# One-hot products for an expert list, and two halves of the tokens' split side by side in one 512-column matmul

## The chip, the cores and the metric

The kernel runs on one core of one Trainium2 chip. The metric is the device time of an execution in microseconds (us). Before the change it is 2601.82 us, the median of three runs (2600.1 to 2602.65).

## What is computed

Two transformer blocks over 256 tokens of width 2048, in float32. The change lies in the part `peer` of the first block, a layer of 16384 small experts: each token chooses 16 experts in each of 8 heads by its scores, takes a gelu of the product of its normed vector with each chosen row of `expert_u`, multiplies by the gates and adds up the chosen rows of `expert_v`.

```python
eidx = e1 * PEER_NKEYS + e2            # 8 heads x 16 experts for a token
gates = jax.nn.softmax(vs, axis=-1)
def block(args):                       # 128 tokens
    xb, ib, gb = args
    act = jax.nn.gelu(jnp.einsum('tkd,td->tk', expert_u[ib], xb))
    return jnp.einsum('tk,tkd->td', act * gb, expert_v[ib])
h = h + peer(rms_norm(h, ffn_norm_gain), w_pq, sub_k1, sub_k2, expert_u, expert_v)
```

## The kernel before

Nothing is gathered for U: all 16384 rows of `expert_u` are read, in 128 steps (`UStep`) of 128 experts, and multiplied with the 256 tokens. What a token hasn't chosen gets a gate of zero. For V only the experts that some token chose are read, by a list.

Float32 products are made of three products in a faster format (float32r): each operand is split into a high part (a copy by ScalarE) and a low part (a subtraction by VectorE), and high x high, high x low and low x high are added in PSUM. The tokens' parts are `xt["h"]` and `xt["l"]`, 16 blocks k of 128 channels x 256 tokens. A step of U works like this, in the order in which it is written, which is the order in which each engine works (`tc.manual_schedule`):

- `prep` of step f+1 comes ahead of the matmuls of step f (`Stream.prep`, look-ahead 1): ScalarE makes the high parts of step f+1 (L818), SyncE loads the rows of step f+2 and VectorE transposes them into `uT` (L808), and VectorE makes the low parts of step f+1 (L823). In the first 64 steps (`NFU`) 8 of the 16 blocks (`NF`) aren't split: they are multiplied in float32, each as two passes (L829). So these steps have one pair of split tiles, the later ones two.
- `mm` of step f: the float32 blocks first, then for each k three products of 256 columns (L834, L835, L836) into the first half of one of three PSUM banks (`ubank`).
- `u_finish` ends gelu for step f-1: a tanh on ScalarE (L849), the last product on VectorE (L850, it reads PSUM) and a DMA of GpSimd's queue into AG in DRAM (L851). Then the first part of gelu for step f: a square on ScalarE (L839) and a product on VectorE (L840).

The tiles `ga` come from a pool of 5 (`t1`) and are free again when their DMA has landed.

After each `mm` a background of generators gets a budget of work (`bg.run`: 2.2 in the first 64 steps, 2.0 in the others; each `yield` says what it cost). It holds, in this order: the top-16 searches for the two halves of the tokens (VectorE mostly), the gates of four groups of 64 tokens (`gate_gen`: one-hots from ScalarE and VectorE, products on TensorE, a copy by ScalarE), their stores (`store_gen`, 16 DMAs of GpSimd's queue each), and `lists_gen`.

`lists_gen` sorts the experts into four classes: chosen by the first 128 tokens alone, by both halves, by the second alone, by none. It computes each expert's place in the list on TensorE, and writes the expert's number to that place of `listD` in DRAM with 128 indirect DMAs of 128 rows (L1121), which GpSimd issues, each with a small memset behind it (L1125). Then the list is read back (L1129), transposed and kept as `listI`.

The V stage runs over blocks of 128 list entries: gathers of AG and `expert_v` by GpSimd's queue (L872, L873), splits, and matmuls of 512 columns (L896 to L898), 24 for a block that serves both halves of the tokens and 12 for one that serves one. `WA, WB0, WB1` say which blocks serve which half: blocks below WA the first, those from WB0 to WB1 the second. If the classes don't fit, a flag is set and a slow loop over the remaining blocks runs behind a `tc.If`.

Of the kernel before, what the change touches and what calls it, by code (L numbers as in the profile page):

```python
# [25 lines left out]
NE = 128  # L26
WB = 4
NF = 8
NFU = 64
WA, WB0, WB1 = 82, 27, 111  # L30

# [58 lines left out]
def tile_kernel(ctx: ExitStack, tc: tile.TileContext, A, out, dbg=None):  # L90
# [20 lines left out]
    def bank(tag):  # L111
        return psp.tile([128, 512], F32, tag=tag, name=tag)
# [155 lines left out]
    xt = {}  # L268

    def new_xt():  # L270
        xt["h"] = xp.tile([128, 16, 256], F32R, tag="xh", name="xh")
        xt["l"] = xp.tile([128, 16, 256], F32R, tag="xl", name="xl")

# [476 lines left out]
    AG = dr.tile([NE * 128, 512], F32, name="AG")  # L750
    listD = dr.tile([NE * 128, 64], F32, name="listD")
# [9 lines left out]
    G.iota(iota, pattern=[[1, 16]], base=0, channel_multiplier=0, allow_small_or_imprecise_dtypes=True)  # L761
    r_bc = tk.tile([128, 256], F32, name="r_bc")
    iotaf = tk.tile([128, 128], F32, name="iotaf")
# [9 lines left out]
    G.iota(pcol, pattern=[[0, 1]], base=0, channel_multiplier=1, allow_small_or_imprecise_dtypes=True)  # L773
    idf = tk.tile([128, 192], F32, name="idf")
    G.iota(idf, pattern=[[128, 192]], base=0, channel_multiplier=1, allow_small_or_imprecise_dtypes=True)
    posU = tk.tile([128, 128], U32, name="posU")
# [3 lines left out]
    gap = tk.tile([1, 1], F32, name="gap")  # L780
    ubank = [bank("acc") for _ in range(3)]
# [5 lines left out]
    class UStep:  # L787
# [38 lines left out]
        def mm(self):  # L826
            acc = ubank[self.f % 3][:, 0:256]
            for k in range(self.nf):
                T.matmul(acc, self.uT[:, k * 128:(k + 1) * 128], xf[:, k, :], start=(k == 0), stop=False)  # L829
            per = (16 - self.nf) // self.nw  # L830
            for k in range(self.nf, 16):
                hi, lo = self.u[(k - self.nf) // per]
                c = slice((k - self.nf) % per * 128, ((k - self.nf) % per + 1) * 128)
                T.matmul(acc, hi[:, c], xt["h"][:, k, :], start=(k == 0), stop=False)  # L834
                T.matmul(acc, hi[:, c], xt["l"][:, k, :], start=False, stop=False)  # L835
                T.matmul(acc, lo[:, c], xt["h"][:, k, :], start=False, stop=(k == 15))  # L836
            u_finish()
            a = t1(F32, "ga")
            S.activation(a, acc, AF.Square)  # L839
            V.scalar_tensor_tensor(a, a, GC1 / GC3, acc, op0=OP.add, op1=OP.mult)  # L840
            pend.append((self.f, acc, a))

    pend = []

    def u_finish():
        if not pend:
            return
        f, x, a = pend.pop()
        S.activation(a, a, AF.Tanh, scale=GC3)  # L849
        V.scalar_tensor_tensor(a, a, 1.0, x, op0=OP.add, op1=OP.mult)  # L850
        G.dma_start(AG[f * 128:f * 128 + 128, 0:256], a)  # L851

    class VStep:
# [12 lines left out]
        def prep(self):  # L866
# [12 lines left out]
            for c in range(2):  # L879
                if self.rest:  # L880
                    hi, lo = [xt[n].rearrange("p k t -> p (k t)")[:, c * 1024:(c + 1) * 1024] for n in "hl"]
# [203 lines left out]
    def lists_gen():  # L1085
# [26 lines left out]
        V.tensor_reduce(pf[:, 0:128], q.rearrange("p a b -> p b a"), AX, OP.add)  # L1112
        V.tensor_copy(posU, pf[:, 0:128])
        V.tensor_scalar(flag[:, 0:1], ps[0:1, 128:129], float(WB0 * 128), None, op0=OP.is_lt)
# [4 lines left out]
        yield 3.0  # L1119
        for f in range(NE):  # L1120
            i = G.indirect_dma_start(out=listD[:, :], out_offset=bass.IndirectOffsetOnAxis(ap=posU[:, f:f + 1], axis=0),  # L1121
                                     in_=idf[:, f:f + 64], in_offset=None)
            tc.declare_no_dep(i.ins, group="list", reason="the rows written are all different")
            tc.add_to_no_dep_group("list", i.ins)
# [422 lines left out]
    def merged_gen(i, j0, j1):  # L1547
        for j in range(j0, j1):
# [6 lines left out]
            k0 = 8 * i + 2 * j  # L1555
            split(flat(xt["h"][:, k0:k0 + 2, :]), flat(xt["l"][:, k0:k0 + 2, :]), pt)
            yield
# [38 lines left out]
```

## Time and profile before

| | before |
|---|---|
| median of 3 runs | 2601.82 us |
| the profiled execution | 2613.04 us |
| its span, from the first to the last instruction | 2611.3 us |
| TensorE busy | 2516.7 us (96%) |
| VectorE busy | 1815.7 us (70%) |
| ScalarE busy | 1315.0 us (50%) |
| GpSimd busy | 554.3 us (21%) |
| granted TensorE clock, mean | 0.986 |

In the rows TensorE is PE (its weight loads PEld), VectorE is DVE, ScalarE ACT, GpSimd POOL, SyncE SP. L834 is line 834 of the kernel. Matmuls overlap, so their durations don't add up: the distance between their starts counts. The same holds, to a lesser degree, for VectorE and ScalarE, where an instruction starts about 0.1 us before the one ahead of it ends. An idle time in brackets names what ended it; "issue" means that the profile shows nothing that the engine waited for.

### The profile page before, as it was taken

How to read it: one execution, taken by the hardware profiler on the slowest of the kernel's cores; microseconds unless marked ns; L12 is line 12 of the kernel's file. 1: busy time of each engine (PE TensorE's matmuls, PEld its weight loads, DVE VectorE, ACT ScalarE, POOL GpSimd, SP SyncE). 2: the span in 40 equal slices, each digit the busy share in tenths (PEclk: the TensorE clock that was granted, in tenths of full speed). 3: DMA queues.
4: the chain of work that ended last, by engine and by line, in shares of the span. 5: the costliest groups of instructions: out<-in, count | busy, mean ns of one | idle time of the engine just before them, and what ended most of it. 6: DMA issues, size and time to landing. Idle time of an engine off the chain costs nothing. (4 is left out here: it accounts for less than half of the span.)

```text
span 2611.3 us, 38031 instructions
## 1 busy us (share of the span) xinstructions
PE 2516.7 (96%) x13895; PEld 2195.1 (84%) x13896; DVE 1815.7 (70%) x2804; ACT 1315.0 (50%) x2169; POOL 554.3 (21%) x789
## 2 busy tenths in 40 slices
PE   9999989999999999998779999999999999999999
PEld 8877779899898999997668888887888888888887
DVE  5665678987979989886447777777665456754564
ACT  6764643254452577543235555555555456544443
POOL 3000000001201112388725555553000000000000
PEclk9999999999999999999789999999999999999999
DMA  6644876565757868696469989987555545555554
GB/s 220 193 129 146 193 165 167 165 168 168 220 144 201 212 176 223 181 241 192 127 241 324 320 321 318 320 317 273 189 191 187 184 163 180 190 178 193 181 193 157
DMA packets 251619, 538.63 MB, mean 206 GB/s; under 512 B 29800, under 2 KB 165952, under 8 KB 236832
## 3 DMA queue, kind: packets, MB, share of 16 engines
q1 hardware_dynamic: 206864, 344.54, 44.4%
q0 software_dynamic: 40992, 189.67, 21.2%
q10 hardware_dynamic: 3568, 1.91, 0.3%
q8 instruction: 111, 1.82, 0.3%
q14 instruction: 84, 0.69, 0.1%
HBM read 494.06 MB, written 41.94 MB: 205 GB/s over the span
## 5 line engine op out<-in xcount | busy, mean ns | idle before, releaser
L120 DVE TENSOR_TENSOR wl<-raw,wh 128x1024 fp32r<-128x1024 f32 (+4 forms) x642 | 740.3, 1171 | 375.8 <-ACT wh L119 341.3
L119 ACT ACTIVATE wh<-raw 128x1024 fp32r<-128x1024 f32 (+4 forms) x642 | 640.1, 1011 | 372.2 <-PE acc L247 279.0
L836 PE MATMUL acc<-xh,wl 128*128 128x256 f32 x1536 | 444.7, 289 | 31.0 <-DVE wl L823 20.7
L245 PE MATMUL acc<-wh,xh 128*128 128x512 f32 (+2 forms) x1152 | 456.7, 396 | 6.0 <-ACT h L406 4.2
L834 PE MATMUL acc<-xh,wh 128*128 128x256 f32 x1536 | 456.0, 297 | 6.1 <-issue 5.5
L835 PE MATMUL acc<-xl,wh 128*128 128x256 f32 x1536 | 441.6, 288 | 9.3 <-issue 8.5
L247 PE MATMUL acc<-wh,xl 128*128 128x512 f32 (+2 forms) x1152 | 447.3, 388 | 0.0
L246 PE MATMUL acc<-wl,xh 128*128 128x512 f32 (+2 forms) x1152 | 446.6, 388 | 0.3 <-DVE wl L120 0.3
L808 DVE STREAM_TRANSPOSE uT<-raw 128x2048 f32<-128x2048 f32 x128 | 295.4, 2308 | 60.5 <-PE acc L829 54.0
L836 PEld LDWEIGHTS acc<-xh,wl 128*128 128x128 f32 x1536 | 300.5, 196 | 39.2 <-DVE wl L823 26.0
L835 PEld LDWEIGHTS acc<-xl,wh 128*128 128x128 f32 x1536 | 301.2, 196 | 11.9 <-issue 10.2
L834 PEld LDWEIGHTS acc<-xh,wh 128*128 128x128 f32 x1536 | 300.9, 196 | 11.8 <-issue 9.9
L245 PEld LDWEIGHTS acc<-wh,xh 128*128 128x128 f32 x1152 | 217.5, 189 | 47.3 <-ACT h L406 4.6
L839 ACT ACTIVATE ga<-acc 128x256 f32<-128x256 f32 x128 | 49.1, 383 | 412.3 <-PE acc L836 325.0
L247 PEld LDWEIGHTS acc<-wh,xl 128*128 128x128 f32 x1152 | 217.3, 189 | 44.0
L246 PEld LDWEIGHTS acc<-wl,xh 128*128 128x128 f32 x1152 | 217.8, 189 | 41.0 <-DVE wl L120 0.7
L818 ACT ACTIVATE wh<-uT 128x1024 fp32r<-128x1024 f32 x192 | 195.1, 1049 | 87.3 <-DVE uT L808 87.2
L829 PE MATMUL acc<-xf,uT 128*128 128x256 f32 x1024 | 234.3, 382 | 3.9 <-ACT h L404 3.9
L823 DVE TENSOR_TENSOR wl<-uT,wh 128x1024 fp32r<-128x1024 f32 x192 | 224.6, 1197 | 7.6 <-ACT wh L818 7.5
L851 POOL DMA_DIRECT2D AG<-ga x128 | 71.1, 556 | 739.4 <-DVE ga L850 723.7
L829 PEld LDWEIGHTS acc<-xf,uT 128*128 128x128 f32 x1024 | 190.9, 191 | 28.2 <-ACT h L404 4.3
L872 POOL DMA_INDIRECT ag<-AG,listI x111 | 142.5, 1284 | 75.9 <-DVE pl L120 51.6
(418 smaller groups left out, 3817.4 us busy)
## 6 DMA issues: line engine op xcount, KB each, us to landing
raw<-in_expert_u_dram SPq DMA_DIRECT2D x1024, 128.0 KB
raw<-in_w_in_dram SPq DMA_DIRECT2D x96, 1024.0 KB
raw<-in_w_out_dram SPq DMA_DIRECT2D x32, 1024.0 KB
raw<-in_w_pq_dram SPq DMA_DIRECT2D x64, 256.0 KB
AG<-ga POOLq DMA_DIRECT2D x128, 128.0 KB
AG<-GB POOLq DMA_DIRECT2D x64, 256.0 KB
raw<-in_w_ple_gate_dram SPq DMA_DIRECT2D x16, 1024.0 KB
raw<-in_w_in_dram SPq DMA_DIRECT2D x16, 544.0 KB
```

The costliest lines, as they stand in the source:

```text
L119: S.activation(hi, src, AF.Copy)
L120: V.tensor_tensor(lo, src, hi.bitcast(F32), op=OP.subtract)
L245: T.matmul(o, xh, hi, start=first, stop=False)
L246: T.matmul(o, xh, lo, start=False, stop=False)
L247: T.matmul(o, xl, hi, start=False, stop=last)
L808: V.transpose(uT.rearrange("p b g j -> p g b j"), self.raw.rearrange("p g (b i) -> p g b i", i=32))
L818: S.activation(hi, self.uT[:, self.nf * 128 + i * n:self.nf * 128 + (i + 1) * n], AF.Copy)
L823: V.tensor_tensor(lo, self.uT[:, self.nf * 128 + i * n:self.nf * 128 + (i + 1) * n], hi.bitcast(F32), op=OP.subtract)
L829: T.matmul(acc, self.uT[:, k * 128:(k + 1) * 128], xf[:, k, :], start=(k == 0), stop=False)
L834: T.matmul(acc, hi[:, c], xt["h"][:, k, :], start=(k == 0), stop=False)
L835: T.matmul(acc, hi[:, c], xt["l"][:, k, :], start=False, stop=False)
L836: T.matmul(acc, lo[:, c], xt["h"][:, k, :], start=False, stop=(k == 15))
```

## The change

- **U's products.** The tokens' high and low parts lie side by side (`xt["x"]`, two tiles of 8 blocks; a class `Half` gives the old views). High part of U times both is one matmul of 512 columns, into a whole bank; low part of U times the high part follows with 256 columns into the bank's first half. The order is: all high products but the last, the float32 blocks, all low products, the last high product.
- **The halves.** ScalarE copies the second half of the bank to a tile `gx`, VectorE adds the first half to it. The square and gelu's two products then work on that tile in SBUF.
- **Gelu's last product** moves from VectorE to GpSimd, as an addition of 1 and a product.
- **Pools.** `t1` has 7 tiles for 5 (two are used per step now); `r_bc` lies in another pool.
- **The list.** The scatter through DRAM goes. An expert's place is split into a high part (block) and a low part (entry), each is made a one-hot by VectorE (comparisons of 8 x 128 columns, result in bf16), ScalarE scales one of them with the expert's row number, and 128 bf16 products on TensorE add up the row numbers in the spare half of the bank `cnt`. The other part of the expert's number, its group f, follows from how many places lie ahead of each group's experts: counts by one-hots and a triangle of ones.
- **Block counts.** `WA, WB0, WB1` are 81, 28, 110 for 82, 27, 111.

The diff, cut to its core:

```diff
-WA, WB0, WB1 = 82, 27, 111
+WA, WB0, WB1 = 81, 28, 110
...
+        xt["x"] = [xp.tile([128, 8, 2, 256], F32R, tag=t, name=t) for t in ("xh", "xl")]
+        xt["h"], xt["l"] = Half(xt["x"], 0), Half(xt["x"], 1)
...
-        return tk.tile([128, 256], dt, tag="t1", name=name, bufs=5)
+        return tk.tile([128, 256], dt, tag="t1", name=name, bufs=7)
...
         def mm(self):
-            acc = ubank[self.f % 3][:, 0:256]
+            bank = ubank[self.f % 3]
+            acc = bank[:, 0:256]
...
+            def high(k):
+                T.matmul(bank, part(k, 0), xt["x"][k // 8][:, k % 8].rearrange("p n t -> p (n t)"),
+                         start=(k == self.nf), stop=(k == 15))
+
+            for k in range(self.nf, 15):
+                high(k)
             for k in range(self.nf):
-                T.matmul(acc, self.uT[:, k * 128:(k + 1) * 128], xf[:, k, :], start=(k == 0), stop=False)
+                T.matmul(acc, self.uT[:, k * 128:(k + 1) * 128], xf[:, k, :], start=False, stop=False)
             for k in range(self.nf, 16):
-                T.matmul(acc, hi[:, c], xt["h"][:, k, :], start=(k == 0), stop=False)
-                T.matmul(acc, hi[:, c], xt["l"][:, k, :], start=False, stop=False)
-                T.matmul(acc, lo[:, c], xt["h"][:, k, :], start=False, stop=(k == 15))
+                T.matmul(acc, part(k, 1), xt["h"][:, k, :], start=False, stop=False)
+            high(15)
             u_finish()
+            u = t1(F32, "gx")
+            S.activation(u, bank[:, 256:512], AF.Copy)
+            V.tensor_tensor(u, acc, u, op=OP.add)
             a = t1(F32, "ga")
-            S.activation(a, acc, AF.Square)
-            V.scalar_tensor_tensor(a, a, GC1 / GC3, acc, op0=OP.add, op1=OP.mult)
-            pend.append((self.f, acc, a))
+            S.activation(a, u, AF.Square)
+            V.scalar_tensor_tensor(a, a, GC1 / GC3, u, op0=OP.add, op1=OP.mult)
+            pend.append((self.f, u, a))
...
         S.activation(a, a, AF.Tanh, scale=GC3)
-        V.scalar_tensor_tensor(a, a, 1.0, x, op0=OP.add, op1=OP.mult)
+        G.tensor_scalar(a, a, 1.0, None, op0=OP.add)
+        G.tensor_tensor(a, a, u, op=OP.mult)
         G.dma_start(AG[f * 128:f * 128 + 128, 0:256], a)
...
-        for f in range(NE):
-            i = G.indirect_dma_start(out=listD[:, :], out_offset=bass.IndirectOffsetOnAxis(ap=posU[:, f:f + 1], axis=0),
-                                     in_=idf[:, f:f + 64], in_offset=None)
-            G.memset(gap, 0.0)
-            if f % 5 == 4:
-                yield 2.0
-        lt = t1(F32, "lt")
-        G.dma_start(GB, listD.rearrange("(b p) o -> b p o", p=128))
-        for _ in range(4):
-            yield 2.0
-        V.tensor_copy(lt[:, 0:128], GB[:, :, 0])
-        pt = bank("ms")
-        T.transpose(pt[:, 0:128], lt[:, 0:128], ident)
-        V.tensor_copy(listI, pt[:, 0:128])
+        def hots(tag, col, n):
+            o = tk.tile([128, 8, 128], BF16, tag=tag, name=tag, bufs=3)
+            V.tensor_tensor(o[:, 0:n], iotaf[:, None, :].to_broadcast([128, n, 128]),
+                            pq[:, col:col + n][:, :, None].to_broadcast([128, n, 128]), op=OP.is_equal)
+            return o
...
+        def products(f0, oa, ob):
+            for j in range(8):
+                T.matmul(lst, ob[:, j], oa[:, j], start=(f0 + j == 0), stop=(f0 + j == NE - 1))
+
+        for f0 in range(0, NE, 8):
+            oa, ob = hots("o1", f0, 8), hots("o2", 128 + f0, 8)
+            S.activation(flat(oa), flat(oa), AF.Copy, scale=pcol)
+            if prev:
+                products(*prev)
+            prev = (f0, oa, ob)
+            yield 2.3
+        products(*prev)
+        V.scalar_tensor_tensor(hf[:, 0:128], hf[:, 128:256], 128.0, lst, op0=OP.mult, op1=OP.add)
+        V.tensor_copy(listI, hf[:, 0:128])
```

Ahead of the loop, left out here, stand some twenty small VectorE operations, two more comparisons (4 x 128 columns) and three short round trips to TensorE, parted by yields of 4.0, 4.0, 1.0 and 2.0; they give the places' two parts and each group's number.

## Rows read from the trace of the kernel before

**Rows 1.** Busy time by stretch: start:end, length, engines' busy us (instructions), clock, DMA.

```profile
399.44:562.99 163.55, 157.21 (x1009) 145.59 (x1008) 147.35 (x286) 54.09 (x103) 12.48 (x23) 1.00 0.63 170
562.99:628.86 65.87, 65.87 (x480) 62.41 (x478) 43.70 (x79) 41.70 (x98) 3.79 (x7) 1.00 0.52 139
628.86:698.52 69.66, 65.77 (x415) 60.55 (x413) 66.59 (x170) 21.80 (x41) 19.79 (x26) 1.00 0.75 219
698.52:773.05 74.53, 74.53 (x543) 70.64 (x541) 53.70 (x98) 47.74 (x113) 4.91 (x9) 1.00 0.58 155
773.05:860.59 87.54, 83.79 (x523) 77.17 (x521) 84.87 (x167) 25.04 (x41) 15.19 (x22) 1.00 0.68 195
860.59:897.23 36.64, 33.30 (x269) 32.82 (x268) 36.05 (x48) 19.75 (x40) 9.49 (x13) 0.95 0.85 228
897.23:1070.42 173.19, 173.19 (x1516) 172.84 (x1514) 157.33 (x240) 130.18 (x274) 27.26 (x40) 1.00 0.75 194
1070.42:1217.92 147.50, 137.37 (x1116) 135.08 (x1115) 121.09 (x130) 59.13 (x92) 111.97 (x181) 0.99 0.83 221
1217.92:1290.37 72.45, 49.99 (x243) 42.45 (x241) 27.23 (x27) 12.90 (x20) 55.32 (x103) 0.74 0.40 112
1290.37:1343.66 53.29, 43.37 (x343) 42.99 (x341) 32.58 (x36) 16.89 (x27) 14.22 (x25) 0.90 0.68 227
...
1357.30:1819.70 462.40, 456.62 (x1980) 373.86 (x1981) 331.98 (x447) 259.14 (x337) 241.23 (x216) 0.99 0.90 318
```

**Rows 2.** ScalarE in order of time, two steps of U: start us, us.

```profile
1110.35 0.38 ACT L839 ACTIVATE ga<-acc 128x256 f32<-128x256 f32 x1 [1.94 <-PE acc L836]
...
1116.11 0.38 ACT L839 ACTIVATE ga<-acc 128x256 f32<-128x256 f32 x1 [3.18 <-PE acc L836]
```

**Rows 3.** TensorE in order of time, products of 256 columns, five apart.

```profile
1103.79 0.28 PE L835 MATMUL acc<-xl,wh 128*128 128x256 f32 x1
...
1104.39 0.28 PE L834 MATMUL acc<-xh,wh 128*128 128x256 f32 x1
```

**Rows 4.** VectorE in order of time, one step of U.

```profile
1111.11 0.42 DVE L850 SCALAR_TENSOR_TENSOR ga<-ga,acc 128x256 f32<-128x256 f32 x1
1111.44 0.42 DVE L840 SCALAR_TENSOR_TENSOR ga<-ga,acc 128x256 f32<-128x256 f32 x1
...
1114.00 2.32 DVE L823 TENSOR_TENSOR wl<-uT,wh 128x1024 fp32r<-128x1024 f32 x2
1116.24 0.42 DVE L850 SCALAR_TENSOR_TENSOR ga<-ga,acc 128x256 f32<-128x256 f32 x1
```

**Rows 5.** Groups of GpSimd, whole span: count, busy us, mean ns, idle before.

```profile
L1121 POOL DMA_INDIRECT listD<-idf,posU x128 | 136.4, 1066 | 30.4 <-issue 30.4
```

**Rows 6.** TensorE in order of time, in the stretch from 1217.92.

```profile
1238.03 0.28 PE L834 MATMUL acc<-xh,wh 128*128 128x256 f32 x1 [0.91 <-issue]
```

**Rows 7.** TensorE in order of time, V stage, products of 512 columns, nine apart.

```profile
1450.48 0.39 PE L896 MATMUL ms<-wh,ph 128*128 128x512 f32 x1
...
1452.54 0.39 PE L896 MATMUL ms<-wh,ph 128*128 128x512 f32 x1
```

**Rows 8.** ScalarE and VectorE in order of time, a square and its product.

```profile
1214.29 0.38 ACT L839 ACTIVATE ga<-acc 128x256 f32<-128x256 f32 x1 [3.69 <-DMA AG<-ga]
...
1214.70 0.42 DVE L840 SCALAR_TENSOR_TENSOR ga<-ga,acc 128x256 f32<-128x256 f32 x1 [0.98 <-ACT ga L839]
```

**Rows 9.** GpSimd in order of time, a product of two tiles.

```profile
18.06 0.46 POOL L444 TENSOR_TENSOR band<-band,ident 128x128 f32<-128x128 f32 x1
```

**Rows 10.** Groups of VectorE, 14 to 33 us (GpSimd at work), then 33 to 160.

```profile
L120 DVE TENSOR_TENSOR wl<-raw,wh 128x704 fp32r<-128x704 f32 x6 | 5.9, 989 | 0.3
...
L120 DVE TENSOR_TENSOR wl<-raw,wh 128x704 fp32r<-128x704 f32 x8 | 7.1, 888 | 0.9 <-ACT wh L119 0.7
```

**Rows 11.** Groups of VectorE, 400 to 1340 us, a comparison with broadcast operands.

```profile
L1017 DVE TENSOR_TENSOR oh<-rf,iota 128x512 f32<-128x512 f32 x16 | 11.0, 685 | 0.2
```

**Rows 12.** TensorE in order of time, start of a step of U.

```profile
1092.87 0.28 PE L834 MATMUL acc<-xh,wh 128*128 128x256 f32 x1
```

More of the change, by code (lines that the diff above doesn't have):

```diff
@@ L268, in tile_kernel, with __init__, __getitem__ @@
     xt = {}
+    class Half:
+        def __init__(self, x, n):
+            self.x, self.n = x, n
+        def __getitem__(self, key):
+            k = key[1]
+            if isinstance(k, slice):
+                return self.x[k.start // 8][:, k.start % 8:(k.stop - 1) % 8 + 1, self.n, key[2]]
+            return self.x[k // 8][:, k % 8, self.n, key[2]]
     def new_xt():
-        xt["h"] = xp.tile([128, 16, 256], F32R, tag="xh", name="xh")
-        xt["l"] = xp.tile([128, 16, 256], F32R, tag="xl", name="xl")
+        xt["x"] = [xp.tile([128, 8, 2, 256], F32R, tag=t, name=t) for t in ("xh", "xl")]
+        xt["h"], xt["l"] = Half(xt["x"], 0), Half(xt["x"], 1)
     def lhs_pair(hi, lo):
@@ L761, in tile_kernel @@
     G.iota(iota, pattern=[[1, 16]], base=0, channel_multiplier=0, allow_small_or_imprecise_dtypes=True)
-    r_bc = tk.tile([128, 256], F32, name="r_bc")
+    r_bc = g2([128, 256], name="r_bc")
     iotaf = tk.tile([128, 128], F32, name="iotaf")
@@ L779, in tile_kernel @@
     flagI = tk.tile([1, 1], I32, name="flagI")
-    gap = tk.tile([1, 1], F32, name="gap")
     ubank = [bank("acc") for _ in range(3)]
@@ L880, in prep @@
                 if self.rest:
-                    hi, lo = [xt[n].rearrange("p k t -> p (k t)")[:, c * 1024:(c + 1) * 1024] for n in "hl"]
+                    both = xt["x"][0].rearrange("p k n t -> p (k n t)")
+                    hi, lo = [both[:, c * 2048 + j * 1024:c * 2048 + j * 1024 + 1024] for j in range(2)]
                 else:
@@ L1119, in lists_gen @@
         yield 3.0
-        for f in range(NE):
-            i = G.indirect_dma_start(out=listD[:, :], out_offset=bass.IndirectOffsetOnAxis(ap=posU[:, f:f + 1], axis=0),
-                                     in_=idf[:, f:f + 64], in_offset=None)
-            tc.declare_no_dep(i.ins, group="list", reason="the rows written are all different")
-            tc.add_to_no_dep_group("list", i.ins)
-            G.memset(gap, 0.0)
-            if f % 5 == 4:
-                yield 2.0
-        lt = t1(F32, "lt")
@@ L1129, in lists_gen @@
-        G.dma_start(GB, listD.rearrange("(b p) o -> b p o", p=128))
-        for _ in range(4):
-            yield 2.0
-        V.tensor_copy(lt[:, 0:128], GB[:, :, 0])
-        pt = bank("ms")
-        T.transpose(pt[:, 0:128], lt[:, 0:128], ident)
-        V.tensor_copy(listI, pt[:, 0:128])
+        tz = t1(BF16, "tz")
+        V.memset(tz[:, 0:3], 0.0)
+        V.tensor_copy(tz[:, 3:7], tot[:, 0:4])
+        st = bank("ms")
+        T.matmul(st[:, 0:4], wt[:, 384:512], tz[:, 3:7], start=True, stop=False)
@@ new lines, in lists_gen @@
+        for c in range(3):
+            T.matmul(st[:, 0:4], wt[:, 512:640], tz[:, 2 - c:6 - c], start=False, stop=(c == 2))
+        pq = g2([128, 264], name="pq")
+        both = g2([128, 264], U32, "pu")
+        V.tensor_copy(both[:, 0:128], pf[:, 0:128])
+        V.tensor_copy(both[:, 128:132], st[:, 0:4])
+        V.tensor_scalar(posU[:, 0], both[:, 0:128], 7, None, op0=OP.logical_shift_right)
+        V.tensor_scalar(posU[:, 1], both[:, 0:128], 127, None, op0=OP.bitwise_and)
+        V.tensor_scalar(both[:, 136:140], both[:, 128:132], 7, None, op0=OP.logical_shift_right)
@@ new lines, in lists_gen @@
+        V.tensor_scalar(both[:, 140:144], both[:, 128:132], 127, None, op0=OP.bitwise_and)
+        V.tensor_copy(pq[:, 0:256], flat(posU))
+        V.tensor_copy(pq[:, 256:264], both[:, 136:144])
+        yield 4.0
+        def hots(tag, col, n):
[3 more added lines that the diff above has]
+            return o
@@ new lines, in lists_gen @@
+        tri = t1(F32, "tri")
+        V.tensor_scalar(tri[:, 0:128], iotaf, pcol, None, op0=OP.is_ge)
+        V.tensor_scalar(tri[:, 128:256], iotaf, pcol, None, op0=OP.is_gt)
+        oa, ob = hots("o1", 256, 4), hots("o2", 260, 4)
+        sp = bank("ms")
+        for c in range(4):
+            T.matmul(sp[:, 0:128], ob[:, c], oa[:, c], start=(c == 0), stop=(c == 3))
+        ss = t1(F32, "st")
+        V.memset(ss[:, 128:129], 1.0)
+        S.activation(ss[:, 0:128], sp[:, 0:128], AF.Copy)
@@ new lines, in lists_gen @@
+        yield 4.0
+        sc = bank("ms")
+        T.matmul(sc[:, 0:1], ss[:, 0:128], ss[:, 128:129], start=True, stop=True)
+        V.tensor_copy(ss[:, 129:130], sc[:, 0:1])
+        yield 1.0
+        sr = bank("ms")
+        T.matmul(sr[:, 0:128], tri[:, 0:128], ss[:, 0:128], start=True, stop=False)
+        T.matmul(sr[:, 0:128], ss[:, 129:130].to_broadcast([128, 128]), tri[:, 128:256], start=False, stop=True)
+        hiU = t1(U32, "hu")
+        hf = t1(F32, "hf")
+        V.tensor_scalar(hf[:, 0:128], sr[:, 0:128], 127.0, None, op0=OP.add)
@@ new lines, in lists_gen @@
+        V.tensor_copy(hiU[:, 0:128], hf[:, 0:128])
+        V.tensor_scalar(hiU[:, 128:256], hiU[:, 0:128], 127, None, op0=OP.bitwise_and)
+        V.tensor_copy(hf[:, 128:256], hiU[:, 128:256])
+        yield 2.0
+        lst = cnt[:, 256:384]
+        prev = None
+        def products(f0, oa, ob):
[8 more added lines that the diff above has]
+            yield 2.3
@@ L1555, in merged_gen @@
             k0 = 8 * i + 2 * j
[L1556 removed]
+            split(xt["h"][:, k0:k0 + 2, :], xt["l"][:, k0:k0 + 2, :], pt.rearrange("p (a b) -> p a b", a=2))
             yield
```

15 lines of the change are left out of this document (6 added, 9 removed).

## The prediction

> **What bounds the kernel now.** I read the stretches first, cut where a U step's first matmul starts, for they tell which engine is full in which part. The reader is to see three pictures in [rows 1]. In the stretches in which gates are built (562.99 to 628.86, 698.52 to 773.05, 897.23 to 1070.42) TensorE is busy to the last nanosecond. In the stretches with top-k work (399.44, 628.86, 773.05, 860.59) VectorE is at 90 to 98% and TensorE has idle time: VectorE sets the pace. From 1070.42 to 1343.66 neither is full: 35 U steps take 273.2 us. Last, the V stage (1357.30 to 1819.70) is TensorE's, 456.6 of 462.4 us.
>
> The steady U step comes next. ScalarE's square of one step and of the next stand 5.76 us apart [rows 2]; 48 products of 256 columns at 0.120 us (five later: 0.60 us) make up just that [rows 3]. On VectorE the same step takes 5.13 us without a gap [rows 4], from one final product (L850) to the next. So TensorE leads by 0.63 us only, and VectorE is the next bound.
>
> The excess of the list part: 35 x 5.76 = 201.6, so 71.6 us are above pure U work. GpSimd's 128 scatters take 1.07 + 0.24 = 1.3 us each with the idle time ahead of them [rows 5], and five of them stand in GpSimd's queue ahead of each U step's store to AG; that is over a U step's time. The five ga buffers run out, and from 1217.92 five steps take 72.45 us instead of 28.8. In that stretch TensorE issues with gaps that have no releaser (0.91 us at 1238.03 [rows 6]), at a granted clock of 0.74 [rows 1]. What those gaps are the trace doesn't say; they begin and end while the scatters run.
>
> **Part by part.** The profiled span is 2611.3 us and its run 2613.04; the median is 2601.82, 11.2 lower. I sum against the span and lay the difference on the median.
>
> *Side-by-side matmul.* Two products of 256 columns cost 2 x 0.120, one of 512 costs 0.229 (nine in 2.06 us [rows 7]): 0.011 us less, 8 times in each of the first 64 steps, 16 in the others. TensorE's step falls from 5.76 to 5.58 (second half) and by 0.09 in the first. The order (high parts first, VectorE's low parts later) gives the low parts more room: they are first needed after 15 wide products (15 x 0.229 = 3.4 us) where they were needed as the third matmul. That smooths, but takes no work off VectorE.
>
> *Halves added.* Per step VectorE loses L850 and gains the addition, 0.33 us each by their spacing [rows 4]: nothing. But a wait is new. The addition must end (0.42), ScalarE must square (0.38), and only then can the next VectorE product start; a hand-over costs 0.03 (ScalarE's square at 1214.29 lasts 0.38, VectorE starts at 1214.70 [rows 8]). So addition to product takes 0.88 instead of 0.33: 0.55 us of empty VectorE per step. Behind it in VectorE's queue stand the top-k or list work, the next transpose and the low parts, on which TensorE waits. Before, a late VectorE found the square ready. Ends: 0 (hidden where VectorE is early) to 0.55; I take 0.55 wherever VectorE is the bound. ScalarE's extra copy (a square's 0.38) finds it busy for a quarter to three quarters of a stretch [rows 1].
>
> *Last product on GpSimd.* Two products of 256 columns; 128 columns cost 0.46 alone [rows 9], so up to 0.92 each, well below a step's time. But beside GpSimd's early work VectorE's 704-column subtraction took 989 instead of 888 ns [rows 10]: 0.10 us each, 0.03 to 0.2 for one or two hits per step. Bounds 0 and 0.92 (blocked for one whole product); I take 0.13, nearest the row. [...]
>
> With 0.68 per step VectorE's busy time in [rows 1] becomes: 147.4 + 23 x 0.68 = 163.0 where 163.55 were taken, so +0.5; 66.6 + 10 x 0.68 = 73.4, +3.7; 84.9 + 13 x 0.68 = 93.7, +6.2; 36.05 + 5 x 0.68 = 39.5, +2.8; 157.3 + 24 x 0.68 = 173.6, +0.4 (TensorE's 173.2 would have fallen to 168.9). The two gate stretches of the first half stay TensorE's: 17 x 0.09 = -1.5.
>
> *The list.* All 128 scatters, the read-back and its transpose go, and with them GpSimd's jam. New on VectorE: 16 x 2 comparisons of 1024 columns. Not in the trace; nearest are the two-input subtraction of 1024 columns, 1.12 by spacing (2.24 for two [rows 4]), and the same comparison with broadcast operands at 512 columns, 0.685 [rows 11]. Bounds 0.685 (the second half free) and 1.37 (twice that); I take 1.10, nearest the subtraction: 35.2 us. It only adds. Small VectorE operations, some 20 of about 0.2 and two comparisons of 512 columns (1.4), with three round trips to TensorE: an estimate of 7, between 4 (the operations alone) and 14 (twice). The first part, the classes, stays; with it the first three steps took 5.2 more than 5.76 each (step 96 starts at 1092.87 [rows 12]; 22.45 - 17.28). VectorE then needs 35 x (5.13 + 0.68) + 35.2 + 7 + 5.2 = 250.8; I add 2 for late loads: 253. TensorE needs 35 x 5.58 + 128 bf16 products (0.06 each, an estimate from half of 0.120) + 8 of waiting for the round trips, 211: hidden. ScalarE's 16 scalings of 1024 columns are hidden too. So 273.2 becomes 253: -20.2. Of the 71.6 us of excess most goes, but some 50 come back as VectorE work.
>
> *Start of V.* Copy, addition and the slower product lengthen the last U step's chain to its store by 0.9 to 2.3: +1.4.
>
> *Block counts.* 81, 28, 110 for 82, 27, 111: blocks for both token halves 53 for 55, for one 57 for 56, so matmuls 53 x 24 + 57 x 12 = 1956 for 1992, 36 x 0.232 (462.4 / 1992) = -8.4, as TensorE is full there. It holds if the counts fit: the reference's selection has 10216 experts in the first half, 3730 in it alone, 13965 in either, within 10368, above 3584, within 14080, so the fallback loop stays off.
>
> Sum: 0.5 + 3.7 + 6.2 + 2.8 + 0.4 - 1.5 - 20.2 + 1.4 - 8.4 = -15.1. The span would be 2596, the median **2587**.
>
> **The rivals.** (1) *VectorE keeps room*: the empty 0.55 is hidden and the ports don't meet. Then the stretches up to 1070.42 give -11 by TensorE's saving (63 steps at 0.09, 29 at 0.18), the list part takes 35 x 5.13 + 47.4 = 227, -46; with +1.4 and -8.4: -64, 2538. For it: the lows have more room in the new order. Against: two hand-overs stand between two VectorE instructions in its own order.
>
> (2) *GpSimd's products block VectorE*, in the 110 steps where VectorE is the bound. If each takes 0.53 instead of 0.13 per step: 110 x 0.40 = +44, 2631. It decides from (15.1 + 5.2) / 110 = 0.18 more, that is 0.31 per step: slower from there. For it: the products come when VectorE subtracts, and 0.92 is possible. Against: the row shows a tenth.
>
> (3) *The gaps on TensorE weren't the scatters'.* Then five steps still take 72.45 instead of 5 x 7.9 = 39.5: +33, 2620. For it: no releaser is named. Against: 1290.37 to 1343.66, with the last scatters, has TensorE busy for 43.4 of 53.3 us again.
>
> That the wide matmul doesn't do what it says is worth little: TensorE isn't the bound in most stretches.
>
> **How the numbers follow.** Forecast 0.55 (2572 to 2602), rival 1 0.18, rival 2 0.19, rival 3 0.08. 0.2%, about what a measurement of this kernel can tell, is 5.2 us. Faster: 0.46 of the forecast and rival 1, 0.64. Same: 0.09 and 0.04 of rival 2, 0.13. Slower: 0.15 and rival 3, 0.23. The range takes in most of rivals 1 and 2: 2545 to 2628.
>
> **What would show it.** Right: no scatters, U steps of the list part at 7 to 8 us with VectorE over 95% busy, ScalarE's square ended by the addition, VectorE's next product ended by the square, the top-k stretches some us longer, V shorter by 8. Rival 1: pure steps at 5.58. Rival 2: 1024-column subtractions well over 1.2 us. Rival 3: gaps without releaser in the list part. Wrong altogether if ScalarE's copy waits on the store of AG (seven buffers, two per step), or if the V part has a second loop.

## The result

The changed kernel takes 2662.68 us (median of four runs, 2662.09 to 2663.36), the kernel before 2601.45: a ratio of 1.0236, 95% interval [1.0218, 1.0253], 61 us slower. Forecast was 2587, with a range of 2545 to 2628.

The stretches of the changed kernel, cut at the same U steps as [rows 1]: searches (top-k work) in the first, third, fifth and sixth, gates in the second, fourth and seventh; the eighth is the list part, U's last 35 steps, and the last line is V, from its first product to its last. Columns: start:end, length, busy us of TensorE, its weight loads, VectorE, ScalarE and GpSimd with their instructions, granted clock, DMA share, GB/s.

```profile
398.87:584.12 185.25, 167.53 (x825) 142.47 (x823) 150.99 (x282) 56.91 (x120) 52.67 (x68) 0.94 0.55 148
584.12:649.42 65.30, 65.30 (x416) 59.21 (x414) 44.50 (x84) 45.99 (x111) 23.00 (x26) 1.00 0.51 146
649.42:726.99 77.57, 69.46 (x334) 57.98 (x332) 69.08 (x171) 22.55 (x47) 35.01 (x44) 0.96 0.75 203
726.99:800.89 73.90, 73.90 (x472) 67.04 (x470) 54.29 (x97) 51.53 (x125) 26.34 (x30) 1.00 0.53 149
800.89:898.32 97.43, 88.33 (x418) 72.97 (x416) 87.62 (x167) 26.99 (x54) 35.75 (x45) 0.96 0.65 176
898.32:937.46 39.14, 32.85 (x189) 27.10 (x187) 35.74 (x43) 19.13 (x41) 19.31 (x22) 1.00 0.76 212
937.46:1124.36 186.90, 172.55 (x1132) 153.51 (x1130) 167.21 (x241) 137.91 (x301) 88.67 (x89) 1.00 0.65 176
1124.36:1388.57 264.21, 226.28 (x1279) 189.68 (x1276) 235.21 (x245) 120.95 (x194) 121.40 (x123) 0.94 0.60 170
1405.39:1872.62 467.23, 461.71 (x1956) 370.54 (x1956) 338.49 (x447) 258.95 (x334) 203.74 (x214) 0.99 0.89 314
```

Against [rows 1], up to step 93 the changed kernel is 54.5 us longer: +21.7, -0.6, +7.9, -0.6, +9.9, +2.5, +13.7. The list part is 9.0 shorter than in the first profile of before, but 1.4 longer than in a second one (below). V starts 3.2 later after U's end and, with 36 products fewer, isn't shorter: the line of V in [rows 1] ends 12 products early (1980 of 1992), and to the start of its last product V takes 465.1 us there, 467.2 here. Neither VectorE nor TensorE is full in the stretches that grew: in the first, VectorE is busy for 151.0 of 185.3 us, where it was 147.4 of 163.6.

What VectorE, ScalarE and TensorE wait for in the first stretch (398.87 to 584.12). Columns: what waited, for what, us in total, times, the longest.

```profile
ACT ga L857 <- DVE gx L855: 105.4, 23, 7.8
...
PE acc L850 <- DVE wl L829: 8.0, 5, 2.4
PE ms L988 <- ACT qT L981: 5.7, 2, 3.0
...
DVE uT L814 <- PE acc L848: 20.3, 5, 8.8
DVE ga L858 <- ACT ga L857: 12.3, 23, 0.5
```

The last line is the wait that was forecast: the product (L858) waits for the square (L857) 0.53 us in each step. The first line is one that the prediction named as a sign but gave no price: the square waits for the addition (L855), 105 us in 23 steps. Before, ScalarE's square waited for TensorE's last product [rows 2]. Now VectorE's addition stands between them, and that stands behind searches, transpose and low parts in VectorE's queue. What ScalarE has to do next (the high parts, the copies of the scores out of PSUM, one-hots for the gates) stands behind the square.

Both waits in one step of the gate stretch: TensorE, VectorE and ScalarE in order of time (start us, us).

```profile
954.38 0.96 PE L842 MATMUL acc<-xh,wh 128*128 128x512 f32 x3 [1.62 <-ACT wh L824]
...
954.36 2.36 DVE L829 TENSOR_TENSOR wl<-uT,wh 128x1024 fp32r<-128x1024 f32 x2 [0.36 <-ACT wh L824]
956.64 0.42 DVE L855 TENSOR_TENSOR gx<-acc,gx 128x256 f32<-128x256 f32 x1
957.60 0.94 DVE L858 SCALAR_TENSOR_TENSOR ga<-ga,gx 128x256 f32<-128x256 f32 x1 [0.55 <-ACT ga L857]
...
955.49 0.36 ACT L854 ACTIVATE gx<-acc 128x256 f32<-128x256 f32 x1
957.15 0.42 ACT L857 ACTIVATE ga<-gx 128x256 f32<-128x256 f32 x1 [1.29 <-DVE gx L855]
...
959.79 1.99 ACT L824 ACTIVATE wh<-uT 128x1024 fp32r<-128x1024 f32 x2
```

ScalarE has the copy (L854) done at 955.85, stands idle until VectorE's addition ends at 957.06, and only then goes on to gate work and to the high parts of the next step, which it starts at 959.79. For the ones before, TensorE waited 1.62 us, until 954.38.

### The profile page after: what moved, and what is told of

Read it like the earlier page. It is cut to its first block, busy times and chain, and to the rows that moved or that the text cites. A ratio compares the mean times of both kernels' runs of the same rounds, so it can differ in the third digit from the quotient of the medians.

```text
span 2661.6 us, 35235 instructions
## 1 busy us (share of the span) xinstructions
PE 2532.2 (95%) x12465; PEld 2117.8 (80%) x12465; DVE 1892.3 (71%) x2851; ACT 1367.8 (51%) x2311; POOL 648.0 (24%) x785
## 3 DMA queue, kind: packets, MB, share of 16 engines
q8 instruction: 99, 1.62, 0.3%
## 5 line engine op out<-in xcount | busy, mean ns | idle before, releaser
L842 PE MATMUL acc<-xl,wh 128*128 128x512 f32 x1024 | 291.3, 411 | 12.0 <-ACT wh L824 8.0
L868 POOL TENSOR_SCALAR ga<-ga 128x256 f32<-128x256 f32 x128 | 147.2, 1150 | 638.4 <-ACT ga L867 350.5
L857 ACT ACTIVATE ga<-gx 128x256 f32<-128x256 f32 x128 | 53.4, 417 | 410.1 <-DVE gx L855 408.5
L829 DVE TENSOR_TENSOR wl<-uT,wh 128x1024 fp32r<-128x1024 f32 x192 | 238.8, 1270 | 6.6 <-ACT wh L824 6.6
L245 PE MATMUL acc<-wh,xh 128*128 128x512 f32 (+1 forms) x576 | 231.2, 401 | 5.8 <-ACT h L416 4.1
L245 PE MATMUL acc<-wh,xl 128*128 128x512 f32 (+1 forms) x576 | 225.5, 391 | 0.0
L247 PE MATMUL acc<-wh,xh 128*128 128x512 f32 (+1 forms) x576 | 224.8, 390 | 0.0
L246 PE MATMUL acc<-wl,xh 128*128 128x512 f32 (+1 forms) x576 | 224.3, 389 | 0.3 <-DVE wl L120 0.3
L247 PE MATMUL acc<-wh,xl 128*128 128x512 f32 (+1 forms) x576 | 222.6, 386 | 0.0
L246 PE MATMUL acc<-wl,xl 128*128 128x512 f32 (+1 forms) x576 | 222.2, 386 | 0.0
L824 ACT ACTIVATE wh<-uT 128x1024 fp32r<-128x1024 f32 x192 | 194.7, 1046 | 12.1 <-DVE uT L814 12.1
L850 PE MATMUL acc<-xl,wl 128*128 128x256 f32 x1024 | 156.4, 296 | 20.8 <-DVE wl L829 20.2
L842 PE MATMUL acc<-xh,wh 128*128 128x512 f32 x512 | 141.5, 421 | 25.0 <-ACT wh L824 24.8
L850 PEld LDWEIGHTS acc<-xl,wl 128*128 128x128 f32 x1024 | 135.9, 193 | 31.6 <-DVE wl L829 28.6
L916 PE MATMUL acc<-wh,ph 128*128 128x512 f32 x324 | 130.3, 402 | 9.0 <-PEq L1550 4.9
```

The costliest lines, as they stand in the source:

```text
L245: T.matmul(o, xh, hi, start=first, stop=False)
L246: T.matmul(o, xh, lo, start=False, stop=False)
L247: T.matmul(o, xl, hi, start=False, stop=last)
L824: S.activation(hi, self.uT[:, self.nf * 128 + i * n:self.nf * 128 + (i + 1) * n], AF.Copy)
L829: V.tensor_tensor(lo, self.uT[:, self.nf * 128 + i * n:self.nf * 128 + (i + 1) * n], hi.bitcast(F32), op=OP.subtract)
L842: T.matmul(bank, part(k, 0), xt["x"][k // 8][:, k % 8].rearrange("p n t -> p (n t)"), start=(k == self.nf), stop=(k == 15))
```

## The experiments

Three theories on the loss in U's first 93 steps were told apart: A, the queues (VectorE empty between addition and product, A1; ScalarE held up by the addition, A2); B, GpSimd's products hold up VectorE (rival 2); C, the transpose waits longer, since the float32 products that read `uT` now come behind seven wide ones. The other runs are on the list and on V's pace. Losses are against [rows 1] unless another run is named.

**lag_square.** In `mm`, behind `u_finish()`, `u_square()` takes the step before:

```diff
             u_finish()
+            u_square()
             u = t1(F32, "gx")
             S.activation(u, bank[:, 256:512], AF.Copy)
             V.tensor_tensor(u, acc, u, op=OP.add)
-            a = t1(F32, "ga")
-            S.activation(a, u, AF.Square)
-            V.scalar_tensor_tensor(a, a, GC1 / GC3, u, op0=OP.add, op1=OP.mult)
-            pend.append((self.f, u, a))
+            sums.append((self.f, u))
...
+    def u_square():
+        if sums:
+            f, u = sums.pop()
+            a = t1(F32, "ga")
+            S.activation(a, u, AF.Square)
+            V.scalar_tensor_tensor(a, a, GC1 / GC3, u, op0=OP.add, op1=OP.mult)
+            pend.append((f, u, a))
...
```

At U's end, left out here, the open steps are finished.

> The changed kernel with the square and gelu's first product of a step issued one step later, behind the next step's products; the last product moves with them. Nothing is left out. Theory A (queues): ScalarE's square waits for VectorE's addition, which stands behind the searches, the transpose and the low parts in VectorE's queue, and ScalarE's copies of the high parts and its other work stand behind that square; this makes most of the 57 us that the changed kernel loses up to step 93. Then the loss up to step 93 falls to 20 us or less, the empty 0.55 us between the addition and the product goes, and the time is 2600 to 2622 us. Theory B (ports): GpSimd's products hold up VectorE; they stay, so 2652 to 2668 us.

Measured: 2593.0 us, ratio to before 0.9963 [0.9948, 0.9977]: 70 us of the change's time are gone, by order alone, 55 of them up to step 93 and most of the rest in the list part. The stretches that answer to the first, seventh and eighth of the changed kernel:

```profile
397.61:563.72 166.11, 155.85 (x825) 134.77 (x823) 149.87 (x281) 62.69 (x125) 49.13 (x66) 1.00 0.65 165
...
899.37:1068.04 168.67, 168.67 (x1132) 152.99 (x1130) 168.31 (x244) 137.53 (x298) 79.91 (x88) 1.00 0.74 198
1068.04:1316.49 248.45, 222.40 (x1279) 188.56 (x1276) 235.91 (x245) 118.89 (x191) 114.73 (x121) 0.95 0.65 179
```

Up to step 93 nothing is lost (-0.6 in all). VectorE is busy for as large a share of the first stretch as before, and the gate stretch is TensorE's again, 4.5 shorter than in [rows 1]: that is the wide matmul's gain, 24 x 0.19. Theory A holds.

**lag_product_only.** As lag_square, but the square stays behind the addition; `u_product()` in the place of `u_square()` has the product alone (the diff is against lag_square):

```diff
             V.tensor_tensor(u, acc, u, op=OP.add)
-            sums.append((self.f, u))
+            a = t1(F32, "ga")
+            S.activation(a, u, AF.Square)
+            sums.append((self.f, u, a))
```

> As lag_square, but ScalarE's square stays where the changed kernel has it, behind the addition in the same step; only VectorE's first product (and the last one) comes a step later. Nothing is left out. So VectorE no longer stands empty for 0.55 us, while ScalarE still waits for VectorE's queue. The changed kernel lost 54.5 us from step 1 to step 93, lag_square none. If VectorE's empty time is the loss (A1): 15 us or less lost to step 93. If ScalarE's wait is the loss (A2): 35 us or more lost there. Seven t1 tiles are just enough for two open steps, so the list part may be longer and is not read.

Measured: 2634.15 us, ratio 1.0127 [1.0107, 1.0147]; 30.3 lost to step 93, between the two. Each theory has its own place. The first, third, fifth and seventh stretch:

```profile
396.28:571.58 175.30, 161.09 (x824) 138.69 (x823) 148.86 (x281) 56.66 (x119) 48.15 (x64) 0.97 0.59 156
636.89:708.58 71.69, 67.63 (x334) 56.95 (x332) 68.50 (x171) 22.16 (x47) 34.93 (x44) 0.98 0.80 214
783.03:872.62 89.59, 84.03 (x417) 71.06 (x416) 86.91 (x167) 26.49 (x53) 35.06 (x46) 1.00 0.73 191
910.79:1097.56 186.77, 174.73 (x1133) 155.56 (x1130) 170.80 (x241) 138.67 (x301) 85.10 (x88) 0.98 0.65 176
```

| us lost against [rows 1] | changed | lag_product_only | lag_square |
|---|---|---|---|
| searches, steps 1 to 24 | 21.7 | 11.8 | 2.6 |
| searches, 32 to 42 | 7.9 | 2.0 | 1.9 |
| searches, 51 to 64 | 9.9 | 2.1 | 1.6 |
| searches, 64 to 69 | 2.5 | 1.5 | -0.8 |
| gates, 69 to 93 | 13.7 | 13.6 | -4.5 |

In the searches of steps 32 to 42 and 51 to 64 VectorE's empty time is the loss: 13.7 of 17.8 us come back with the product moved, 0.6 per step in 23 steps. In steps 1 to 24 it is about half. In the gates moving the product alone gives nothing back, and the waits there say why (us in total, times, the longest; the first two lines are of the changed kernel, the others of lag_product_only):

```profile
DVE ga L858 <- ACT ga L857: 13.3, 24, 0.8
DVE wl L829 <- ACT wh L824: 6.1, 11, 0.9
...
DVE wl L829 <- ACT wh L824: 15.6, 13, 1.4
...
ACT ga L858 <- DVE gx L856: 41.6, 24, 2.7
```

The 13.3 us of waiting for the square are gone from VectorE, but it waits 9.5 more for ScalarE's high parts (L824), and these stand behind the square, which still waits 41.6 us for VectorE (46.5 in the changed kernel). Another 3.6 go into VectorE's own work (170.8 us for 167.2): 17 of that stretch's 120 comparisons for the gates took 0.82 to 0.83 us, where 0.34 is usual, all 17 while GpSimd's product ran. Only with the square moved too (lag_square) does VectorE wait for neither, and is busy for 168.3 of 168.7 us.

**product_on_vector.** The rival: GpSimd.

```diff
-        G.tensor_scalar(a, a, 1.0, None, op0=OP.add)
-        G.tensor_tensor(a, a, u, op=OP.mult)
+        V.scalar_tensor_tensor(a, a, 1.0, u, op0=OP.add, op1=OP.mult)
```

> The changed kernel with gelu's last product back on VectorE as one instruction, as before the change. VectorE gains 0.34 us of work per step and loses what it waits beside GpSimd (1024-column subtractions and the first product together 25 us over 128 steps in the trace, 0.19 per step). Theory B (ports) as the main cause: faster than the changed kernel, 2640 us or less. Theory A (queues): VectorE is longer by 0.15 per step in some 90 steps, so 2665 to 2685 us.

Measured: 2673.52 us, ratio 1.0271 [1.0254, 1.0288], 11 slower than the changed kernel. So GpSimd's products aren't the cause: with the last product back on VectorE the loss is larger.

**float32_early.** Theory C.

```diff
-            for k in range(self.nf, 15):
-                high(k)
+            high(self.nf)
             for k in range(self.nf):
                 T.matmul(acc, self.uT[:, k * 128:(k + 1) * 128], xf[:, k, :], start=False, stop=False)
+            for k in range(self.nf + 1, 15):
+                high(k)
```

> The changed kernel with the float32 blocks of the first 64 steps behind the first wide product and not behind all seven, so that the tile of transposed rows is free some 1.4 us earlier, as before the change. Theory C (VectorE's transpose waits for these products): the loss from step 1 to 64 falls from 38 us to 28 or less, the time to 2652 or less. Theory A: the transpose waits only where VectorE is early anyway, so 2657 to 2668.

Measured: 2656.68 us, ratio 1.0211 [1.0191, 1.0232]. From step 1 to 64 the loss falls from 38.3 to 30.3 us: 8 us are the order's, where theory C expected 10 or more: a part of the loss but a small one, and most of it (5.7) lies in steps 1 to 24. There VectorE's transpose waits 11.4 us for the float32 products, where the changed kernel has 20.3 (above).

**list_alone.** The kernel before, with the new list and block counts and seven `t1` tiles, and nothing of U's change.

```diff
-WA, WB0, WB1 = 82, 27, 111
+WA, WB0, WB1 = 81, 28, 110
-        return tk.tile([128, 256], dt, tag="t1", name=name, bufs=5)
+        return tk.tile([128, 256], dt, tag="t1", name=name, bufs=7)
...
-        for f in range(NE):
-            i = G.indirect_dma_start(out=listD[:, :], out_offset=bass.IndirectOffsetOnAxis(ap=posU[:, f:f + 1], axis=0),
...
+        for f0 in range(0, NE, 8):
+            oa, ob = hots("o1", f0, 8), hots("o2", 128 + f0, 8)
...
```

> The kernel before with the list by one-hot products, the new block counts and seven t1 tiles; U's products and gelu as before. By the prediction's own terms VectorE needs 35 x 5.13 + 35.2 + 7 + 5.2 = 227 us in the list part where 273 were taken, and V is 8.4 shorter: 2545 to 2560 us. If the five long steps were not the scatters' doing (rival 3), 33 more: 2578 to 2593. If V's products take 233 ns here too as in the changed kernel and not 229, 8 us more than the first.

Measured: 2581.59 us, ratio 0.9921 [0.9904, 0.9937]: a gain of 20 us. Every stretch up to step 93 is as in [rows 1] within 0.2 us, the list part takes 240.2, 13 over the sum of the prediction's terms; V takes 466.3. The time is one that was expected if rival 3 held, but the stretches speak against it: no step of that part takes more than 10.2 us.

**wide_alone.** The changed kernel with the scatters of before.

```diff
-        for f0 in range(0, NE, 8):
-            oa, ob = hots("o1", f0, 8), hots("o2", 128 + f0, 8)
...
+        for f in range(NE):
+            i = G.indirect_dma_start(out=listD[:, :], out_offset=bass.IndirectOffsetOnAxis(ap=posU[:, f:f + 1], axis=0),
...
```

> The changed kernel with the list by scatters as before; the wide products, the addition of the halves, GpSimd's product and the block counts stay. Theory A or B (the loss is U's gelu chain): the same 57 us up to step 93, then a list part of 273 us or some 5 longer, 2660 to 2680 us. If the list's work had caused the loss, 2600 to 2620.

Measured: 2709.82 us, ratio 1.0414 [1.0396, 1.0431]. To step 93 the loss is as in the changed kernel (54.3 us), but the list part takes 320.8, where 273 to 278 were expected. Who waits in 1311.87 to 1396.65, nine steps of 9.4 us:

```profile
ACT ga L861 <- POOL ga L873: 58.8, 9, 6.8
DVE ga L862 <- ACT ga L861: 37.1, 9, 4.1
```

ScalarE's square needs a tile that GpSimd's last product (L873) sets free, and that product stands behind five scatters. So the change's two parts depend on each other: GpSimd's product costs this much as long as the scatters stand in the same queue.

**before_again.** The kernel before, a second profile.

> The kernel before, unchanged, for a second profile of it. Its first profiled run took 2613.0 us, 11.2 over the median, and list_alone gains 32 us against that span but 20 against the median, with every stretch up to step 93 equal. If the 11 us lie in the list part with the scatters: this run takes about 2602 us and its list part about 262 us where the first had 273.2, all other stretches within 1 us. If they lie elsewhere, the list part is 273 again.

Measured: 2601.03 us. Its list part:

```profile
1068.72:1331.52 262.80, 220.23 (x1697) 215.50 (x1695) 181.95 (x191) 89.01 (x139) 184.79 (x308) 0.92 0.73 201
```

262.8 us where the first profile had 273.2, all other stretches within 0.2: the 11 us by which that profile lay over the median were in the scatters' part, which differs from run to run: here one step takes 28.3 us and no other more than 10.9, where the first profile has five of 13 to 17. Against this run the changed kernel's list part is 1.4 us longer, not 9.0 shorter.

**list_alone_pad, list_alone_pad64, list_alone_pad_behind.** An unused tile of 72 floats (288 bytes) or 16 floats (64 bytes) ahead of the `t1` tiles; in the third, 8 floats behind them.

```diff
+    V.memset(tk.tile([128, 72], F32, name="pad"), 0.0)
```

> list_alone with an unused tile of 72 floats, which shifts the tiles allocated behind it by 288 bytes, to where wide_alone has them (there V's 1956 products took 457.7 us; in list_alone and in the changed kernel 466.3 and 467.2). If the place of the tiles sets the pace of V's products: V takes 458 us, the time is 2573 us. If it is what the new list leaves behind (its contents or its work): V stays at 466, 2582.

> list_alone with a tile of 16 floats: a shift of 64 bytes. V's products took 466.3 us unshifted and 458 to 459 shifted by 32 and by 288 bytes. If it is the place within 64 bytes that counts: 466. If any shift does it: 458.

> list_alone with a tile of 8 floats placed behind the t1 tiles: ph and pl (V's weights) keep their place, the gathered gates ag, uT and the rest are shifted by 32 bytes. If it is the place of ph and pl that counts: V takes 466 us. If it is that of ag and the others: 458.

Measured: 2573.44 us for the first, ratio 0.9891 [0.9872, 0.991], V 458.1 us; the others 2582.43 and 2581.33 us in one run each, V 465.2 both times. 400 us inside V in list_alone, then in list_alone_pad (columns as above; the first count in brackets is TensorE's products):

```profile
1340.00:1740.00 400.00, 400.00 (x1716) 321.81 (x1715) 291.83 (x387) 225.58 (x290) 183.47 (x194) 1.00 0.91 317
```

```profile
1340.00:1740.00 400.00, 400.00 (x1749) 327.86 (x1748) 295.82 (x395) 225.96 (x296) 186.77 (x197) 1.00 0.92 324
```

1716 against 1749 products in the same time, TensorE full and at full clock in both: 233.1 and 228.7 ns each. The place of the tiles of `ph` and `pl`, V's weights, sets it: with a shift of 64 bytes, or with only the tiles behind them shifted, 1716 products again go through in the same 400 us.

**lag_vector_pad32.** lag_square with the last product on VectorE (as in product_on_vector) and a tile of 8 floats.

> lag_square with gelu's last product on VectorE, and a tile of 8 floats that shifts what is allocated behind it by 32 bytes. Theory B (ports): in lag_square VectorE still loses 0.19 us per step beside GpSimd; without GpSimd's products it loses nothing but has 0.33 us more work, so the VectorE-bound steps are 0.14 longer: 5 to 12 us longer over U than lag_square. If GpSimd's products cost nothing: 0.33 x 75 to step 93 and 0.33 x 25 behind it, 33 us longer. V: 458 us if an odd multiple of 32 bytes is what matters, 466 if it needs the whole 288.

Measured: 2586.12 us, ratio 0.9936 [0.9915, 0.9957]; V 459.2. Its first stretch and its list part:

```profile
400.49:569.40 168.91, 158.30 (x825) 135.31 (x823) 154.43 (x302) 61.77 (x125) 11.41 (x21) 0.99 0.57 161
...
1080.14:1321.22 241.08, 218.35 (x1279) 185.81 (x1276) 230.08 (x277) 118.27 (x191) 33.51 (x51) 0.97 0.66 184
```

Against lag_square the first three search stretches are 9.8 us longer (2.8 + 3.1 + 3.9, in 46 steps), 0.21 per step: VectorE has 0.33 more to do, so GpSimd's products had cost it 0.12 there. In the list part it is the other way: 7.4 us shorter in 35 steps, so GpSimd's had cost 0.54 per step, more than VectorE's own product. VectorE's busy time there says the same: 230.1 us, where lag_square has 235.9 without that product. Over all of U it is 1.9 us longer, less than expected, since the two nearly cancel. A shift of 32 bytes is enough for V's better pace.

**mixed.** The first 64 steps as before the change, the others as in lag_vector_pad32.

```diff
+            if self.nf:
...
+                for k in range(self.nf, 16):
+                    T.matmul(acc, part(k, 0), xt["h"][:, k, :], start=False, stop=False)
+                    T.matmul(acc, part(k, 0), xt["l"][:, k, :], start=False, stop=False)
+                    T.matmul(acc, part(k, 1), xt["h"][:, k, :], start=False, stop=(k == 15))
+                u_finish()
+                sums.append((self.f, acc))
+                u_square()
+                return
```

> A version to beat both. The first 64 steps as before the change (three products of 256 columns, square from PSUM, VectorE's last product); the other 64 with the wide products, the addition of the halves, square and first product one step later, the last product on VectorE; the new list; a tile of 8 floats that shifts what lies behind it by 32 bytes. By the stretches of the runs so far: nothing lost up to step 64 (list_alone: 0.0), 6 gained from 64 to 93 and 32 in the list part (lag_vector_pad32), V shorter by 6: 44 in all, 2556 to 2562 us. If the first and the second half of the steps disturb each other where they meet, up to 5 more.

Measured: 2567.59 us, ratio 0.9873 [0.9853, 0.9893], the fastest of all. The expected 44 us were reckoned against the first profile of before; against before_again the stretches give 35 (3.3 and 4.4 in steps 64 to 93, 20.4 in the list part, 6.7 in V), as measured; 2556 to 2562 us were expected.

## Why the prediction was wrong

*What bounds the kernel before* stood where it was tried: in lag_square the gate stretch falls by what TensorE saves, and in lag_vector_pad32 the first three search stretches get longer when VectorE has more to do. Up to step 93, 12.1 us were forecast and 54.5 measured.

*Halves added: the size was right, the sum was not.* Addition to product was forecast at 0.88 us (its terms, 0.42 + 0.38 and two hand-overs of 0.03, make 0.86) and takes 0.96 in the searches, so 0.62 of empty VectorE per step where 0.55 was taken. The step that failed is the one behind it: 147.4 + 23 x 0.68 = 163.0, "so +0.5", where 21.7 were measured. It lets VectorE's 16 us of idle time in that stretch take up the new work. Half of it was two waits of 5.0 and 3.2 us, in steps in which the transpose waits for TensorE or for its rows; the new empty time comes in every step, and work behind it in VectorE's queue doesn't move into those waits. From the wait list of VectorE in that stretch, kernel before, second profile:

```profile
DVE uT L808 <- PE acc L829: 8.7, 4, 5.0
DVE uT L808 <- DMA raw<-in_expert_u_dram: 3.9, 4, 3.2
```

Eight waits make up 12.6 of the 16 us. In the changed kernel they weren't used up but grew (20.3 us in five). In the search stretches at 628.86 and 773.05 [rows 1] the same step failed: 3.7 and 6.2 forecast, 7.9 and 9.9 measured, of which 13.7 is empty time that lag_product_only takes away.

*ScalarE's queue was left out.* The prediction asked what stands behind the product in VectorE's queue, and of ScalarE only how busy it is ("a quarter to three quarters of a stretch"). It didn't ask what stands behind the square in ScalarE's own queue. It put that term at nothing. Moving the square behind the product's move gives back 18 us in the gates (13.6 to -4.5 in the table) and 9 in steps 1 to 24; forecast were +0.4 for the gates. TensorE was full there, so VectorE's 0.68 was weighed against TensorE, and a third engine held them both up.

*A stall of TensorE cost more than its length.* The granted clock of the search stretches fell from 1.00 to 0.94 and 0.96. In step 3, TensorE and ScalarE in order of time:

```profile
419.47 2.07 PE L850 MATMUL acc<-xl,wl 128*128 128x256 f32 x8 [2.41 <-DVE wl L829]
...
426.14 2.93 PE L988 MATMUL ms<-GB,qT 128*128 128x128 f32 x12 [2.96 <-ACT qT L981]
...
425.19 0.42 ACT L857 ACTIVATE ga<-gx 128x256 f32<-128x256 f32 x1 [2.80 <-DVE gx L855]
425.51 0.58 ACT L981 ACTIVATE qT<-ms 128x512 f32<-128x512 f32 x1
```

The eight low products behind the gap of 2.41 us take 2.07 us, where seven spacings of 0.120 and a last product of 0.28 [rows 3] make 1.12: from 419.47 to 421.54 the granted clock is 0.50, and 0.50 again in the 2.93 us behind the gap of 2.96. The gap of 2.96 us ends with ScalarE's copy `qT` (L981), and that stood behind the square, which had waited 2.80 us for VectorE's addition. Steps 3 and 4 together lost 11.2 us (17.73 + 12.74 for 10.26 + 9.06); in lag_product_only they still lose 9.5, in lag_square 0.4. The prediction kept the clock out of its sum.

*Rival 2* gave 2631 by VectorE blocked beside GpSimd and decided from 0.31 per step. By lag_vector_pad32 the price is 0.12 in the searches, where 0.13 had been taken, and 0.54 in the list part, so it is real, but product_on_vector shows that it isn't why the change is slower. Single instructions lost more than the 0.10 us of [rows 10]: the product at 957.60 (above) takes 0.94 us where 0.42 is usual, while GpSimd's product (L869) runs from 957.52 for 0.74. From the groups of VectorE and of GpSimd during U:

```profile
L829 DVE TENSOR_TENSOR wl<-uT,wh 128x1024 fp32r<-128x1024 f32 x192 | 238.8, 1270 | 6.6 <-ACT wh L824 6.6
...
L858 DVE SCALAR_TENSOR_TENSOR ga<-ga,gx 128x256 f32<-128x256 f32 x128 | 62.9, 491 | 68.1 <-ACT ga L857 68.1
```

```profile
L868 POOL TENSOR_SCALAR ga<-ga 128x256 f32<-128x256 f32 x127 | 146.4, 1152 | 638.4 <-ACT ga L867 350.5 <-DVE vsel L1001 138.8 <-DVE mr L1003 76.5
```

The subtraction's mean was 1197 ns before and is 1270; the product's is 491 for 426 undisturbed, by 16 of 128 that took 0.92 to 0.94, all 16 while GpSimd's product (L869) ran. GpSimd's addition takes 0.85 alone and 1.15 on the mean: in part of the steps it is GpSimd that takes longer. The runs show these times; what the two engines share ("ports" in rival 1 and in the expectations) they don't show.

*Rival 1* fell: the empty time wasn't hidden, and its list part of 227 us was 240.2 in list_alone, which has no such empty time. *Rival 3* fell: in list_alone, with the scatters gone, the longest step of that part takes 10.2 us, where five took 72.45 in all.

*The list.* The comparison of 1024 columns costs 1.13 us by spacing (two in 2.27, 1254.74 to 1257.01), where 1.10 was taken. In the steps with comparisons U goes at 8.18 us, as 5.13 + 0.68 + 2.20 = 8.01 would have it. The part took 264.2 for 253: steps 93 to 99, classes and round trips, took 61.1 us, 21 over seven pure steps, of which the prediction had 12. The new chain of hand-overs has its share here too, since lag_square took 248.5. And -20.2 was reckoned against the first profile, whose list part was 10 us over that of the second; laying the 11.2 between span and median on the median was the mistake, since those 11 us lay in the part that the change takes out.

*Start of V*: +1.4 forecast, +3.2 measured. The last step's copy, addition, square, product and tanh end at 1390.87; then GpSimd's addition takes 0.84 and its product 1.76 us, beside subtractions of VectorE, where 0.74 is usual. The store is issued at 1393.96, 5.4 us behind TensorE's last product, where it was 2.1 before.

*Block counts.* -8.4 forecast. wide_alone, where the weights lie as well as before, has it: 457.7 for 465.1 us, -7.4. In the changed kernel the tiles lie otherwise and 1956 products at 4.4 ns more each take it back (8.6).

In sum, from the second profile of before: 54.5 to step 93, 1.4 in the list part, 3.0 at V's start and 2.2 in V make 61.1 us; the medians differ by 61.2.

## What to carry over

Where two engines hand a step to and fro, ask for both queues what stands behind the instruction that now waits, also for the engine that is half idle. Idle time summed over a stretch is no room for new work unless it lies in the steps that need it: count it step by step. A chain with two hand-overs can cost next to nothing if its second half is issued a step later, behind work that is ready anyway: here -0.6 us for 54.5 up to step 93.

## What was not expected of the hardware

V's products of 512 columns went at 233.1 ns (1716 in 400 us, in the changed kernel, list_alone, list_alone_pad64 and list_alone_pad_behind) or at 228.7 (1749, in wide_alone, list_alone_pad and mixed; 1750 in the kernel before), by where their weights lie in SBUF. By the programs' allocation the address of the first `t1` tile, in which the weights lie, is a multiple of 64 bytes in the four slow programs (149952; 150016 with 64 bytes of padding) and lies 32 bytes beyond one in the fast ones (141024 in the kernel before, 149984 in mixed and lag_vector_pad32, 150240 in wide_alone and list_alone_pad). The other operand, `wh` and `wl`, lies 32 bytes beyond one in all of them, so whether the weights' own place counts or their place against the other operand's isn't shown.

VectorE's subtraction and product, which took up to 1.76 us for 1.18 and 0.94 for 0.42 beside GpSimd in the changed kernel, read two tiles each. Its comparisons for the gates read one tile and two columns of numbers, and yet 17 of 120 took 0.82 to 0.83 us for 0.34 while GpSimd's product ran, in the gate stretch of lag_product_only.
